# A hybrid decoder layer: the causal mask of the attention scores set by GpSimd's selections in SBUF, in place of identity products in PSUM

## The chip, the cores and the metric

The kernel runs on one core of a Trainium2 chip. Five engines work side by side, each through its own queue in order: TensorE (PE; its weight loads are shown apart, as PEld), VectorE (DVE), ScalarE (ACT), GpSimd (POOL) and SyncE (SP), which here issues the transfers. They wait for each other through semaphores. The metric is the time of the whole kernel on the device in microseconds, the median of several runs.

## The reference

One decoder layer on 512 tokens of 1024 channels: a half-step SwiGLU, a mixer of two halves that read the same normed input (a gated linear recurrence on 512 channels, stick-breaking attention with 8 heads of 64), an output projection, and a second half-step SwiGLU. What the change touches is the attention:

```
z = q @ k.T                                   # one head, one block of 128 queries
causal = k_pos[None, :] < q_pos[:, None]      # a key strictly before the query
log_beta = log_sigmoid(z)
log_1m = where(causal, log_sigmoid(-z), 0.0)
tail = cumsum(log_1m, reverse=True) - log_1m  # what the later keys left of the stick
w = where(causal, exp(log_beta + tail), 0.0)
out = w @ v
```

The weight of a key is thus sigmoid(z) times the product of sigmoid(-z) over the keys between it and the query. A key at or after the query has weight 0 and breaks nothing off: its sigmoid(-z) counts as 1.

## The kernel before

All matrix products are taken in three parts (high by high, high by low, low by high), so that float32 precision is kept; the helper `mm3` issues the three. The layer goes in stages: the first SwiGLU, the projections and the recurrence, the attention together with both halves of the output projection, the second SwiGLU. PE works nearly without a pause through all of them.

The attention (lines 566 to 705) has 24 steps. The heads go in pairs, and a pair goes in three units: query block 3 (512 keys), query block 2 (384 keys), and blocks 1 and 0 together (256 and 128 keys). `weigh` (line 575) computes a unit for both heads: PE forms the scores of each block in a PSUM bank `pz` from three products (line 589; each head has 64 rows of the array, so the two heads' products run beside each other). Then PE adds the mask: an identity in bf16 times the tile `fut_b` adds -1e30 to the last 128 columns of a block where the key is at or after the query (line 598). ScalarE turns the bank into `s` = sigmoid(-z) (line 603; two buffers) and `be` = sigmoid(z) (line 605; five buffers). DVE scans `s` from the last key backwards by multiplication into `rest` (line 608), one scan for each block, and multiplies `be` by it (line 618). With -1e30 in PSUM `s` is 1 and `be` is 0 for the keys that don't count.

`turn_weights` (line 621) transposes a head's weights on PE (line 626) and ScalarE copies them into `wt` (line 636). `attend` (line 639) multiplies them by the values, and `take` (line 651) prepares the result for the output projection (`yal`, line 656, on DVE; the squares, line 160, on ScalarE, summed on POOL, line 161).

The order is written out by hand in part. WEIGH names the steps behind which the next unit's scores are issued; FILL those behind which a block of the recurrent half's output projection fills PE: `project_out` (line 555), whose weights are split by ScalarE (line 121) and DVE (`l_o`, line 123), whose result DVE scales (`yo`, line 563) and POOL adds to x (line 564); REST names the steps that the last such blocks wait for. When the kernel is built, a planner works through all instructions with costs of its own and a priority by the order of the program, and lays down the order of each engine's queue; so each queue's order can change when instructions come or go.

The constants are made at the start (lines 90 to 112): `fut` is a zero tile in which POOL sets -1e30 by one selection (line 106), and DVE casts it and the identity to bf16 (lines 110 and 112).

Of the kernel before, what the change touches and what calls it, by code (L numbers as in the profile page):

```python
# [12 lines left out]
ALU = mybir.AluOpType  # L13
# [14 lines left out]
RG_C = 8.0  # L28
CHUNKS = [8, 7, 7]  # blocks of the hidden width between two partial down projections
WARM = 9  # products that only start the tensor engine's clock  # L30
# Attention goes in 24 steps, each of which turns a block row of one head's weights. The
# steps behind which the next weights are computed, those behind which a block of the
# recurrent half's output projection fills the tensor engine, and those that the
# blocks left over wait for:
WEIGH = (1, 4, 5, 7, 9, 10, 13, 15, 16, 19)
FILL = (4, 8, 12, 16)
REST = (18, 23, 23)

# columns of the packed per-channel vectors
C_G1, C_GM, C_G2 = 0, 8, 16  # L40
# [6 lines left out]
def hybrid_layer_kernel(  # L47
# [25 lines left out]
    def psum(name, **tags):  # L73
        """The eight PSUM banks, cut into the given tags."""
        if banks:
            banks.pop("stack").close()
        banks["stack"] = ExitStack()
        banks["pool"] = banks["stack"].enter_context(
            tc.tile_pool(name=f"ps_{name}", bufs=1, space=PSUM, reuse_waits="tile")
        )  # L80
        banks["tags"] = tags
# [5 lines left out]
    def bank(name, tag="b"):  # L87
        return banks["pool"].tile([P, T], F32, tag=tag, name=name, bufs=banks["tags"][tag])

# [1 line left out]
    mhalf = const.tile([P, 8], F32, tag="mhalf", name="mhalf")  # L91
# [10 lines left out]
    make_identity(nc, ident)  # L102
    # keys at or after the query
    fut = const.tile([P, P], F32, tag="fut", name="fut")
    nc.vector.memset(fut, 0.0)
    nc.gpsimd.affine_select(
        out=fut, in_=fut, pattern=[[-1, P]], compare_op=ALU.is_gt, fill=-1e30, base=0, channel_multiplier=1
    )
    ident_b = const.tile([P, P], BF16, tag="ident_b", name="ident_b")
    nc.vector.tensor_copy(ident_b, ident)  # L110
    fut_b = const.tile([P, P], BF16, tag="fut_b", name="fut_b")
    nc.vector.tensor_copy(fut_b, fut)

    x = [xpool.tile([P, T], F32, tag=f"x{k}", name=f"x{k}") for k in range(KD)]

# [1 line left out]
    def weights(src, name, n=KD * P):  # L117
# [16 lines left out]

# [1 line left out]
    class Normed:  # L136
# [26 lines left out]
        def rsqrt(self, dim):  # L163
            """[tokens, block] 1/sqrt(mean + eps)."""
            n = self.name
            pt = bank(f"pst_{n}", "y")
            for b in range(NB):
                self.summed = nc.tensor.matmul(  # L168
                    pt[:, b : b + 1],
                    self.acc[:, b * P : (b + 1) * P],  # L170
                    ones[:, 0:1],
                    start=True,
                    stop=True,
                )
            m = stat.tile([P, NB], F32, tag="m", name=f"m_{n}")
            nc.vector.tensor_scalar(
                m, pt[:, 0:NB], 1.0 / dim, EPS, op0=ALU.mult, op1=ALU.add
            )
            r = stat.tile([P, NB], F32, tag="r", name=f"r_{n}")
            nc.gpsimd.tensor_tensor(r, m, mhalf[:, 0:NB], op=ALU.pow)  # L180
            self.r = r

        def spread(self):
            """The same along the free axis, on every partition."""
            n, r = self.name, self.r
            pt = bank(f"psr_{n}", "y")
            for b in range(NB):
                self.spreading = nc.tensor.transpose(  # L188
                    pt[:, b * P : (b + 1) * P], r[:, b : b + 1].to_broadcast([P, P]), ident
                )  # L190
            rb = stat.tile([P, T], F32, tag="rb", name=f"rb_{n}", bufs=1)
            nc.scalar.copy(rb, pt)
            self.rb = rb

# [1 line left out]
    def ffn(name, xn, wg, wu, wd, first, done):  # L196
# [59 lines left out]

    # ================= first FFN =================
    psum("ffn_a", b=6, y=2)
    # the tensor engine's clock rises only after some microseconds of work
    pt = bank("warm")  # L260
# [4 lines left out]
    def first_products():  # L265
        """Channels 0..255, in the order in which x and the weights arrive."""
        with tc.tile_pool(name="first", bufs=1, reuse_waits="tile") as fi:
# [52 lines left out]

    # ================= token mixer =================
    mix = ctx.enter_context(ExitStack())
    mp = mix.enter_context(tc.tile_pool(name="mix", bufs=2, reuse_waits="tile"))

    # -4 log_sigmoid(lambda) per channel, with log1p by its series: u = exp(-|lambda|),
    # v = u / (1 + u) = sigmoid(-|lambda|), w = u / (2 + u) = v / (2 - v).
    lam = vec[:, C_LAM : C_LAM + NJ]
# [33 lines left out]

# [1 line left out]
    rnn = ExitStack()  # L363
# [5 lines left out]
    def project(j, between=None):  # L369
        """[128 channels, tokens] of the input projection, before the norm's factor."""  # L370
        pts = []
        for c, n in ((j, "xr"), (NJ + j, "ga")):
            wh, wl = weights_early(w_rg[c], f"{n}{j}")
            pt = bank(f"p{n}{j}")
            for k in range(KD):
                s = slice(k * P, (k + 1) * P)
                mm3(pt, wh[:, s], wl[:, s], nm.h[k], nm.l[k], k == 0, k == KD - 1)
            pts.append(pt)
            if between and n == "xr":
                between()  # L380
        return pts

    def convolve(j, pr, pg):
# [17 lines left out]
        conv.append((xc, xch, xcl))  # L401
        # gelu(g) = g * sigmoid(2 sqrt(2/pi) (g + 0.044715 g^3))
        g2 = rp.tile([P, T], F32, tag="g2", name=f"g2{j}")
# [8 lines left out]
    def gate(j):  # L412
# [5 lines left out]
        mm3(px, bxh[:, s], bxl[:, s], xch, xcl, True, True)  # L418
        # a = exp(-s), tau = tanh(s / 2): sqrt(1 - a^2) = sqrt(tau) (1 + a)
        nc.scalar.activation(dec[:, j, :], pa, AF.Sigmoid, bias=v1(C_BA + j))  # L420
# [11 lines left out]
    def recur():  # L432
        # one change of the activation tables for each function
        with tc.issue_after(box["gate"].ins):
# [26 lines left out]

# [1 line left out]
    qkT = {}  # L463
# [89 lines left out]

# [1 line left out]
    def project_out(k, c, yh, yl, norm, tag, after=None):  # L555
# [9 lines left out]

# [1 line left out]
    # A head's weights are held as [keys, queries], a block of 128 keys every W columns,  # L567
    # from the first query block that sees it on.
    W = 3 * P
    with tc.tile_pool(name="att", bufs=2, reuse_waits="tile") as ap:  # L570
# [4 lines left out]
        def weigh(qbs, pair):  # L575
            """What each key gets: its part of the stick, of what the later keys left."""
            pzs = [bank(f"pz{qbs[0]}_{h}", "z") for h in pair]
            col = 0
            parts = []
            for qb in qbs:  # L580
# [4 lines left out]
                for a, b in (("qh", "kh"), ("qh", "kl"), ("ql", "kh")):  # L585
                    with tc.issue_after(both.ins) if both else nullcontext():
                        for pz, h in zip(pzs, pair):
# [5 lines left out]
                                start=a + b == "qhkh",  # L593
                                stop=False,
                            )
                # from the query on: weight 0, nothing broken off
                for pz in pzs:
                    nc.tensor.matmul(pz[:, col + n - P : col + n], ident_b, fut_b, start=False, stop=True)
                col += n
            for pz, h in zip(pzs, pair):  # L600
# [4 lines left out]
                nc.scalar.activation(be[:, :col], pz[:, :col], AF.Sigmoid)  # L605
                rest = ap.tile([P, T], F32, tag="rest", name=f"rest{u}")
                for c, n in parts:
                    nc.vector.tensor_tensor_scan(
                        rest[:, c : c + n - 1][:, ::-1],
                        s[:, c + 1 : c + n][:, ::-1],  # L610
                        zero.to_broadcast([P, n - 1]),
                        1.0,
                        op0=ALU.mult,
                        op1=ALU.add,
                    )
# [23 lines left out]
        def attend(pair, py, ws):  # L639
            """[channels of the pair, queries]; the heads in different columns of the array"""  # L640
            for b in range(NB):
# [59 lines left out]
        for k in range(KD):  # L701
            # the norm's own small products go ahead of all but the first blocks
            after = None if k < 2 else na.summed if k == 2 else na.spreading
# [3 lines left out]

    # ================= second FFN =================
    psum("ffn_b", b=6, y=2)
# [9 lines left out]
def _layout(x, ffn1_norm, ffn1_w_gate, ffn1_w_up, ffn1_w_down, mix_norm, w_in,  # L719
# [8 lines left out]
    def by_block(w):  # L728
        # [K, N] -> [N/128][p, k, m]: stationary blocks of 128 columns
        k, n = w.shape  # L730
# [59 lines left out]
```

## Time and profile before

| | us |
|---|---|
| median of three runs | 957.67 (957.35 to 958.53) |
| span of the profiled execution, first to last instruction | 953.7 |
| PE busy in the span | 938.0 (98%), 4267 products |
| DVE busy | 524.2 (55%) |
| ACT busy | 331.3 (35%) |
| POOL busy | 124.3 (13%) |

For the profiled execution only its span is known; the median of the timed runs is 4.0 us above it. The profile holds every instruction with its engine, its line, the tiles that it writes and reads, its start and its duration, the idle time of its engine in front of it and what ended that. Busy time of PE counts a product from its start to its modelled end, and products overlap, so a busy PE is not PE at its peak. Durations of POOL are rough. Where several equal instructions follow each other, the timeline puts them in one row with their count, and the duration is that of the whole row.

### The profile page before, as it was taken

How to read it: one execution, taken by the hardware profiler on the slowest of the kernel's cores; microseconds unless marked ns; L12 is line 12 of the kernel's file. 1: busy time of each engine (PE TensorE's matmuls, PEld its weight loads, DVE VectorE, ACT ScalarE, POOL GpSimd, SP SyncE). 2: the span in 40 equal slices, each digit the busy share in tenths (PEclk: the TensorE clock that was granted, in tenths of full speed). 3: DMA queues.
4: the chain of work that ended last, by engine and by line, in shares of the span. 5: the costliest groups of instructions: out<-in, count | busy, mean ns of one | idle time of the engine just before them, and what ended most of it. 6: DMA issues, size and time to landing. Idle time of an engine off the chain costs nothing. (4 is left out here: it accounts for less than half of the span.)

```text
span 953.7 us, 10714 instructions
## 1 busy us (share of the span) xinstructions
PE 938.0 (98%) x4267; PEld 764.9 (80%) x4267; DVE 524.2 (55%) x679; ACT 331.3 (35%) x476; POOL 124.3 (13%) x87
## 2 busy tenths in 40 slices
PE   8999999999999999999899998999999999999998
PEld 6888888888888888888776576888888888888887
DVE  7655334554354556765859949554534545345542
ACT  7232222322222244346456645322212222222220
POOL 4000000000000022552911239100000000000000
PEclk9999999999999999999999999999999999999999
DMA  7222322222322233222110013223232232322331
GB/s 243 92 108 90 109 89 93 106 78 100 111 96 100 78 103 111 96 91 79 67 56 12 24 66 126 96 94 106 71 128 89 91 101 59 131 107 89 95 115 55
DMA packets 29425, 89.32 MB, mean 94 GB/s; under 512 B 3392, under 2 KB 5696, under 8 KB 29376
## 3 DMA queue, kind: packets, MB, share of 16 engines
q1 hardware_dynamic: 29376, 88.65, 27.0%
q8 instruction: 33, 0.54, 0.2%
q14 instruction: 16, 0.13, 0.0%
HBM read 86.54 MB, written 2.10 MB: 93 GB/s over the span
## 5 line engine op out<-in xcount | busy, mean ns | idle before, releaser
L132 PE MATMUL pgb<-xl_b,h_gb 128*128 128x512 f32 x176 | 68.9, 392 | 2.8 <-DVE xl_b L147 2.7
L132 PE MATMUL pdb<-hlb,h_db 128*128 128x512 f32 (+1 forms) x183 | 69.4, 381 | 0.0
L133 PE MATMUL pdb<-hhb,l_db 128*128 128x512 f32 (+1 forms) x183 | 69.1, 381 | 0.0
L132 PE MATMUL pub<-xl_b,h_ub 128*128 128x512 f32 x176 | 69.0, 392 | 0.0
L133 PE MATMUL pub<-xh_b,l_ub 128*128 128x512 f32 x176 | 69.0, 392 | 0.0
L131 PE MATMUL pdb<-hhb,h_db 128*128 128x512 f32 (+1 forms) x183 | 68.9, 381 | 0.0
L131 PE MATMUL pub<-xh_b,h_ub 128*128 128x512 f32 x176 | 68.9, 391 | 0.0
L133 PE MATMUL pgb<-xh_b,l_gb 128*128 128x512 f32 x176 | 68.7, 391 | 0.0
L131 PE MATMUL pgb<-xh_b,h_gb 128*128 128x512 f32 x176 | 68.7, 390 | 0.0
L132 PE MATMUL pda<-hla,h_da 128*128 128x512 f32 x176 | 68.1, 389 | 0.0
L133 PE MATMUL pda<-hha,l_da 128*128 128x512 f32 x176 | 67.8, 389 | 0.0
L131 PE MATMUL pda<-hha,h_da 128*128 128x512 f32 x176 | 67.7, 389 | 0.0
L131 PE MATMUL pga<-xh_a,h_ga 128*128 128x512 f32 x160 | 62.4, 390 | 0.0
L132 PE MATMUL pua<-xl_a,h_ua 128*128 128x512 f32 x160 | 62.3, 390 | 0.0
L133 PE MATMUL pga<-xh_a,l_ga 128*128 128x512 f32 x160 | 62.3, 389 | 0.0
L131 PE MATMUL pua<-xh_a,h_ua 128*128 128x512 f32 x160 | 62.3, 389 | 0.0
L133 PE MATMUL pua<-xh_a,l_ua 128*128 128x512 f32 x160 | 62.2, 389 | 0.0
L132 PE MATMUL pga<-xl_a,h_ga 128*128 128x512 f32 x160 | 62.2, 389 | 0.0
L161 POOL TENSOR_TENSOR sqa_m<-sqa_m,sq_m 128x512 f32<-128x512 f32 x7 | 11.4, 1626 | 330.4 <-issue 312.1
L248 DVE SCALAR_TENSOR_TENSOR x<-pdb,x 128x512 f32<-128x512 f32 (+1 forms) x25 | 16.6, 669 | 68.6 <-PE pdb L133 68.6
L121 ACT CAST h_ga<-r_ga 128x1024 fp32r<-128x1024 f32 x24 | 25.3, 1053 | 79.6 <-issue 34.4
L227 DVE TENSOR_TENSOR uub<-pub,rb_b 128x512 f32<-128x512 f32 x22 | 15.2, 691 | 67.4 <-PE pub L133 67.4
(278 smaller groups left out, 2101.3 us busy)
## 6 DMA issues: line engine op xcount, KB each, us to landing
r_gb<-in_wg SPq DMA_DIRECT2D x22, 512.0 KB, 3.1
r_ub<-in_wu SPq DMA_DIRECT2D x22, 512.0 KB, 3.2
r_ga<-in_wg SPq DMA_DIRECT2D x20, 512.0 KB, 3.2
r_ua<-in_wu SPq DMA_DIRECT2D x20, 512.0 KB, 3.1
r_da<-in_wd SPq DMA_DIRECT2D x16, 448.0 KB, 3.3
r_db<-in_wd SPq DMA_DIRECT2D x16, 448.0 KB, 3.3
r_da<-in_wd SPq DMA_DIRECT2D x8, 512.0 KB, 3.5
r_o<-in_w_out SPq DMA_DIRECT2D x16, 256.0 KB, 2.5
```

Of the source, the lines that this page charges most:

```text
L121: nc.scalar.copy(hi, raw)
L131: nc.tensor.matmul(out_, wh, ah, start=start, stop=False)
L132: nc.tensor.matmul(out_, wh, al, start=False, stop=False)
L133: nc.tensor.matmul(out_, wl, ah, start=False, stop=stop)
L161: nc.gpsimd.tensor_add(self.acc, self.acc, sq)
L227: nc.vector.tensor_mul(u, pu, rb)
L248: nc.vector.scalar_tensor_tensor(x[k][:, t], pt[:, t], 0.5, x[k][:, t], op0=ALU.mult, op1=ALU.add)
```

## The change

The tiles `fut`, `ident_b` and `fut_b` go, and with them a memset, a selection and two casts at the start, and the mask's products in `weigh`; the last of the three score products now closes the bank. When ScalarE has written a head's `s` and `be`, POOL sets the last 128 columns of each block in both tiles by an affine selection in place: where the key is not before the query, `s` becomes 1 and `be` becomes 0. The scans and multiplications then follow as they did. (Comments that the change drops are left out here.)

```diff
-    fut = const.tile([P, P], F32, tag="fut", name="fut")
-    nc.vector.memset(fut, 0.0)
-    nc.gpsimd.affine_select(
-        out=fut, in_=fut, pattern=[[-1, P]], compare_op=ALU.is_gt, fill=-1e30, base=0, channel_multiplier=1
-    )
-    ident_b = const.tile([P, P], BF16, tag="ident_b", name="ident_b")
-    nc.vector.tensor_copy(ident_b, ident)
-    fut_b = const.tile([P, P], BF16, tag="fut_b", name="fut_b")
-    nc.vector.tensor_copy(fut_b, fut)
...
                                 start=a + b == "qhkh",
-                                stop=False,
+                                stop=a + b == "qlkh",
                             )
-                for pz in pzs:
-                    nc.tensor.matmul(pz[:, col + n - P : col + n], ident_b, fut_b, start=False, stop=True)
                 col += n
...
                 rest = ap.tile([P, T], F32, tag="rest", name=f"rest{u}")
+
+                for c, n in parts:
+                    for t, fill in ((s, 1.0), (be, 0.0)):
+                        d = t[:, c + n - P : c + n]
+                        nc.gpsimd.affine_select(
+                            out=d, in_=d, pattern=[[-1, P]], compare_op=ALU.is_gt,
+                            fill=fill, base=0, channel_multiplier=1,
+                        )
                 for c, n in parts:
                     nc.vector.tensor_tensor_scan(
```

## Rows read from the trace of the kernel before

**Rows 1.** The page: its first line, the busy time of each engine with share and count, and the span in 40 equal slices of 23.8 us (each digit the busy share in tenths; PEclk the granted clock).

```profile
span 953.7 us, 10714 instructions
PE 938.0 (98%) x4267; PEld 764.9 (80%) x4267; DVE 524.2 (55%) x679; ACT 331.3 (35%) x476; POOL 124.3 (13%) x87
...
PE   8999999999999999999899998999999999999998
...
DVE  7655334554354556765859949554534545345542
...
POOL 4000000000000022552911239100000000000000
PEclk9999999999999999999999999999999999999999
```

**Rows 2.** A table of the attention by stretch: the stretch and its length, then for PE, PEld, DVE, ACT and POOL in this order the busy us and the instructions in brackets, then the granted clock, the share of the transfer engines and GB/s. The first row is the whole stage.

```profile
497.40:553.50 56.10, 52.60 (x323) 34.77 (x323) 51.33 (x79) 39.07 (x91) 10.75 (x8) 1.00 0.07 24
497.40:507.00 9.60, 7.70 (x54) 4.70 (x54) 8.33 (x10) 6.66 (x15) 1.70 (x2) 1.00 0.08 27
507.00:524.00 17.00, 16.86 (x101) 11.38 (x101) 16.55 (x30) 11.88 (x29) 2.28 (x2) 1.00 0.05 16
524.00:538.00 14.00, 12.57 (x82) 7.92 (x81) 12.02 (x16) 10.11 (x24) 3.93 (x3) 1.00 0.11 39
538.00:549.00 11.00, 10.97 (x64) 6.88 (x63) 10.25 (x15) 6.28 (x16) 1.64 (x1) 1.00 0.05 19
```

**Rows 3.** The same table over the stage, for the scans of line 608 alone and for the multiplications of line 618 alone (DVE).

```profile
497.40:553.50 56.10, 27.33 (x32) 1.00 0.07 24
...
497.40:553.50 56.10, 17.87 (x32) 1.00 0.07 24
```

**Rows 4.** Who waited for whom in the stage: the waiting engine, tile and line, whom it waited for, the us in total, the number of waits and the longest.

```profile
ACT s L603 <- DVE rest L608: 6.8, 8, 1.8
...
PE pw L626 <- DVE be L618: 3.2, 3, 1.5
...
DVE rest L608 <- ACT s L603: 2.6, 4, 1.0
```

**Rows 5.** The timeline of the first microseconds: the first and the last of DVE's steps for the mask's constants, and ScalarE's first work on an input.

```profile
1.01 0.17 DVE L105 MEMSET fut<- 128x128 f32 x1
...
1.57 0.23 DVE L112 CAST fut_b<-fut 128x128 bf16<-128x128 f32 x1
...
4.29 0.72 ACT L145 ACTIVATE xh_a<-x,vec 128x512 fp32r<-128x512 f32 x1 [2.07 <-DMA x<-in_xT]
```

**Rows 6.** The mask's products: all of them (shortest, median and longest in ns, first and last start), their busy time in the stage on PE and PEld, and PE's timeline around the first pair of them.

```profile
L598 PE MATMUL pz<-fut_b,ident_b x32: 219/224/230, 498.4 to 549.1; 128*128 128x128 bf16 x32
...
497.40:553.50 56.10, 4.56 (x32) 1.82 (x32) 1.00 0.07 24
...
497.80 0.40 PE L589 MATMUL pz<-kTl,qTh 64*128 64x512 f32 x2
498.03 0.40 PE L589 MATMUL pz<-kTh,qTl 64*128 64x512 f32 x2
498.36 0.29 PE L598 MATMUL pz<-fut_b,ident_b 128*128 128x128 bf16 x2
498.58 0.44 PE L589 MATMUL pz<-kTh,qTh 64*128 64x384 f32 x1
```

**Rows 7.** Groups of POOL's instructions by line and form: busy us, mean ns of one, idle time before them. First the two selections of the whole kernel, then the additions to x in the stage.

```profile
masks.py:199 POOL TENSOR_SCALAR_AFFINE_SELECT ident<-ident 128x128 f32<-128x128 f32 x1 | 0.3, 293 | 0.1
L106 POOL TENSOR_SCALAR_AFFINE_SELECT fut<-fut 128x128 f32<-128x128 f32 x1 | 0.3, 292 | 0.0
...
L564 POOL TENSOR_TENSOR x<-x,yo 128x512 f32<-128x512 f32 x5 | 8.2, 1648 | 39.7 <-DVE yo L563 39.7
```

**Rows 8.** The timeline of POOL and of DVE around 514 us: a POOL instruction with two inputs beside DVE instructions with two inputs in SBUF. The multiplication of the same form at 500.59 stands last, for comparison; POOL was idle then.

```profile
513.71 1.64 POOL L564 TENSOR_TENSOR x<-x,yo 128x512 f32<-128x512 f32 x1 [8.98 <-DVE yo L563]
...
513.55 0.68 DVE L123 TENSOR_TENSOR l_o<-r_o,h_o 128x512 fp32r<-128x512 f32 x1
514.14 1.76 DVE L618 TENSOR_TENSOR be<-be,rest 128x511 f32<-128x511 f32 x1
...
500.59 0.69 DVE L618 TENSOR_TENSOR be<-be,rest 128x511 f32<-128x511 f32 x1
```

**Rows 9.** The same around 391 us, where POOL's instruction has one input tensor (line 406), and all instructions of line 406 (shortest, median and longest in ns).

```profile
389.61 0.77 POOL L390 TENSOR_SCALAR xc<-xr,vec 128x512 f32<-128x512 f32 x1 [6.21 <-DVE xr L386]
390.85 0.80 POOL L406 TENSOR_SCALAR g<-g 128x512 f32<-128x512 f32 x1 [0.47 <-ACT g L404]
...
390.41 0.75 DVE L394 SCALAR_TENSOR_TENSOR xc<-xr,vec,xc 128x512 f32<-128x512 f32 x1 [0.32 <-POOL xc L390]
...
391.20 0.98 DVE L394 SCALAR_TENSOR_TENSOR xc<-xr,vec,xc 128x512 f32<-128x512 f32 x1
...
L406 POOL TENSOR_SCALAR g<-g x4: 619/800/1182, 390.8 to 417.9; 128x512 f32<-128x512 f32 x4
```

**Rows 10.** The timeline of the stage, rows of ACT, DVE and POOL that show how one waits for the other: the first unit, a sum of squares, and the last double unit.

```profile
498.63 0.60 ACT L603 ACTIVATE s<-pz 128x512 f32<-128x512 f32 x1 [0.67 <-PE pz L598]
...
499.26 1.22 DVE L608 TENSOR_TENSOR_SCAN rest<-s,zero 128x511 f32<-128x511 f32 x1 [0.57 <-ACT s L603]
...
499.60 0.61 ACT L603 ACTIVATE s<-pz 128x512 f32<-128x512 f32 x1
...
501.19 1.22 DVE L608 TENSOR_TENSOR_SCAN rest<-s,zero 128x511 f32<-128x511 f32 x1
...
534.67 0.60 ACT L160 ACTIVATE sq_t<-py 128x512 f32<-128x512 f32 x1 [1.39 <-DVE yal L656]
...
535.34 1.27 POOL L161 TENSOR_TENSOR sqa_t<-sqa_t,sq_t 128x512 f32<-128x512 f32 x1 [1.79 <-ACT sq_t L160]
...
549.26 0.49 ACT L603 ACTIVATE s<-pz 128x384 f32<-128x384 f32 x1
549.65 0.49 ACT L605 ACTIVATE be<-pz 128x384 f32<-128x384 f32 x1
...
549.79 1.00 DVE L608 TENSOR_TENSOR_SCAN rest<-s,zero 128x255 f32<-128x255 f32 x2 [0.23 <-ACT s L603]
```

## The prediction

> **What bounds the kernel now.** I read the page first: its busy shares and its strip of 40 slices [rows 1]. TensorE (PE) is busy for 98% of the span, at a granted clock of nine tenths or more in every slice, that is at 2.4 GHz. It is the only engine near its limit over the whole kernel. But the share is a mean. VectorE (DVE) is at 55% overall but at nine tenths in the two slices (501 to 548 us) that hold most of the attention, where GpSimd (POOL) is at one and two tenths. So I read the attention alone, as a table by stretch [rows 2]. In its 56.10 us PE is busy for 52.60 and DVE for 51.33, and PE's clock stands at 1.00. The idle time of PE lies in two stretches (1.90 us in the first, 1.43 in the third), that of DVE is 4.77 in all. The two engines are within 1.3 us of each other, so this stage has no spare engine but ACT (39.07) and POOL (10.75). What DVE does there is almost all scans (27.33 us) and the multiplications behind them (17.87) [rows 3], exactly the work that the change touches.
>
> Then the waits of the stage [rows 4]. ScalarE waits 6.8 us for a scan to give back one of the two `s` buffers, PE waits 3.2 us for `be` from a multiplication, and DVE waits 2.6 us (4 times) for `s`. DVE is waited for more than it waits. The path goes to and fro: DVE paces from 497 to 507 and from 524 to 538, where PE stands idle, PE in the stretches between, where it doesn't [rows 2], and at the end the last scans and turns pace again. Whatever is added to DVE in this stage shows within about a microsecond; what is taken from PE shows only as far as DVE has idle time to give back.
>
> **The change part by part.** *The constants.* `fut`, `ident_b`, `fut_b` go: one memset, one selection and two casts between 1.0 and 1.8 us. The first input is not there before 4.29 us (ScalarE's first scaled copy starts there, after a wait for its load), so this is worth nothing [rows 5].
>
> *The identity products.* 32 products go (8 heads times 4 query blocks), each with its weight load. They have 4.56 us of busy time, at 0.22 us each, and overlap. In time on PE a pair of heads costs 0.22 us: the pair starts at 498.36 and the next product at 498.58 [rows 6]. The load of the identity also sits idle until the 64-row products before it are through: the last of these start at 498.03, and such products follow each other at 0.23 us (497.80, 498.03; all in [rows 6]), so without the pair the next could start at 498.26 in place of 498.58, 0.32 us sooner. 16 pairs times 0.22 to 0.32 are 3.5 to 5.1 us of PE. ScalarE's `s` can start sooner by the same amount.
>
> *The selections.* In their place come 64 (8 heads, 4 blocks, `s` and `be`), each 128 by 128 f32 in place on POOL. The trace has this very instruction twice, at 0.29 us [rows 7]. 64 times 0.29 are 18.7 us; POOL goes from 10.75 to about 29.4 of 56.1 us, far from a bound. The price is what they do to DVE. Where POOL runs beside a DVE instruction with two SBUF inputs, the trace shows turns, not sharing [rows 8]: POOL adds to x from 513.71 to 515.35; the subtraction that DVE had begun keeps its 0.68 us, the multiplication that starts at 514.14 takes 1.76 in place of 0.69, 1.07 more, for an overlap of 1.21. So DVE loses the overlap less 0.14, and for a whole selection at most 0.29 less 0.14, 0.15 us. Nearer to a selection are POOL's instructions with one input [rows 9]. The one at 390.85 ends at 391.65; DVE's at 391.20 takes 0.98 in place of 0.75, so it loses 0.23 of an overlap of 0.45. Its base is 0.62 (its shortest), and it ended 0.49 behind the DVE instruction that it had waited for, so 0.13 of it passes in the wait. By these a waiting selection ends 0.29 - 0.13 = 0.16 us after DVE's instruction, and the next of DVE would lose 0.16 less 0.22, nothing. The bounds are thus 0 and 0.15 us for each; the far end is its whole 0.29. I take 0.06, nearer to the row with one input: 64 times 0.06 = 3.8 us, bounds 0 and 9.6.
>
> The Trainium skill (SBUF — State Buffer, section Who interferes with whom) states that a DVE instruction with two SBUF inputs and a GpSimd instruction that reads SBUF exclude each other, and that whichever issues second blocks fully until the first is done. The turns in [rows 8] agree, with 1.07 us lost of 1.21. By that rule without any overlap the 64 selections would cost 18.7 us in place of 3.8, an estimate of 976 us for the kernel.
>
> *The new wait.* The scan no longer waits for ScalarE alone but for POOL behind it. Behind a waiting scan stand, in DVE's order, its multiplication, the next head's scan, and the `l_o` and `yo` steps of the output projection that fills PE; PE's turns wait for them. Most of this is hidden: `s` is usually there 1 to 2 us before its scan (done at 500.21 for the scan at 501.19) [rows 10]. Where DVE already waits for `s`, the selection adds POOL's start 0.07 us after ScalarE's end (535.27, 535.34), 0.29 for itself and DVE's start 0.03 later (390.38, 390.41 in [rows 9]), some 0.39 us in place of 0.03 (499.23, 499.26), and the removed products give 0.22 to 0.32 back: up to 0.14 for each of 4 waits, 0.5 us. In the double unit (blocks 1 and 0) POOL's order is `s`, `be`, `s`, `be`: the second scan waits for the third selection, which stands behind a `be` that ScalarE delivers 0.39 us after `s` (549.26, 549.65), while DVE scanned both blocks in 1.00 us without a pause. For 8 heads: 0 if ScalarE is ahead, three selections at 0.16 plus 0.10 = 0.58 if not; I take 0.2, 1.6 us (bounds 0 and 4.6). Selections also queue behind the five additions to x, 1.65 us each, that POOL runs in the stage [rows 7]; DVE loses most of those already today, so only the selection itself comes on top: 0 to 5 times 0.29, I take 0.5 us.
>
> *What is given back.* DVE has 4.77 us of idle time. Of this the waits for `s` shrink when DVE comes later or PE sooner. In the stretches that PE paces, DVE's idle time is 0.45 and 0.75 us [rows 2], so at most 1.2 of PE's gain passes on; in 524 to 538 it is 1.98, which added work partly fills. I take 2.8 back of 4.77; the start of the stage (0.57) and the short gaps of 0.1 us between a scan and its own multiplication remain.
>
> *Sum.* 3.8 + 0.5 + 1.6 + 0.5 - 2.8 = +3.6 us, with bounds of about -3 (no loss to the turns, no exposed wait, 3 us given back) and +15. The profiled execution has a span of 953.7 us, the median of the three runs is 957.67, 4.0 us more that lie around the span and don't change. 957.7 + 3.6 = 961.3 us.
>
> **The rivals.** *PE's gain wins (faster).* If a selection fits into the gap of 0.1 us that DVE leaves between a scan and its multiplication (500.48 in [rows 10], 500.59 in [rows 8]), and into DVE's instructions that read PSUM, DVE loses nothing, and the earlier `s` takes away most of DVE's waits. DVE's 51.33 us plus some 1.8 of unavoidable gaps are then the floor, 53.1 in place of 56.1: -3 us, 954.7. For it speaks the one-input row; against it that DVE's gaps are few and that PE's own wait is only 3.5 us. It decides when a selection costs DVE under about 0.02 us and no scan waits. *A draw.* The added DVE time of 3 to 4 us is met by idle time and by the shorter PE queue; 957.7, within 1.9. *DVE is shut out for longer.* If each selection costs 0.15, as the two-input rows would have it, 5.8 us more than in my sum: 967.1; up to 976 at the whole 0.29. For it speaks that most DVE work in the stage has two SBUF inputs, the scan among them; against it the smaller loss beside one-input instructions. The skill's rule, named above, is this rival without the overlap. *It does not shorten PE.* If the change from 64-row to 128-row weights costs the same behind the scores anyway, PE gains 0.22 and not 0.32 for a pair; as DVE paces, that moves the sum by under 1 us and stays in the forecast. The order of all queues is laid out again by the planner when the kernel is built; a different place for a block of output projection could move any of these by 1 to 2 us, and the range holds that.
>
> **How the numbers follow.** Forecast, DVE paces and loses some: 0.45, at 961.3. Shut out for longer: 0.13, at 967. Draw: 0.22. PE's gain wins: 0.20, at 954.7. A measurement of this kernel can tell about 0.2% (1.9 us) from no change. So slower has 0.58, same 0.22, faster 0.20. The range goes from 955.0 to 968.0: it leaves out the lower half of the fast case (0.1) and the upper half of the shut-out case with a rest of the forecast (0.1). Within the forecast alone it would be 959.6 to 965.
>
> **What would show it.** In the changed profile: 64 selections on POOL near 0.29 us when alone and up to over 1 us where they wait behind a scan; scans and multiplications that are longer than their shortest by 0.05 to 0.15 in the mean (now 27.33 and 17.87 us in sum); DVE's waits named after POOL's selections in place of ScalarE; PE's wait for `be` above 3.2 us; the stage longer than 56.1 by 3 to 4 us, and nothing outside it changed. The forecast is wrong if DVE's sum in the stage stays below 53, if PE's idle time in it falls, or if the loss comes from POOL's queue (scans waiting behind additions to x) and not from turns with DVE.

## The result, and the profile after

The changed kernel takes 959.21 us (median of 20 runs, 958.44 to 961.44), the kernel before 957.66 in the same comparison (20 runs, 955.52 to 959.24). The ratio is 1.0018, with a 95% interval of 1.0012 to 1.0025: about 1.7 us slower (1.1 to 2.4 by the interval). The forecast was 3.6 us slower.

The two profiled spans differ by more, 957.0 against 953.7. The later runs list span and time of each execution side by side, and they differ by 1.7 to 1.9 us in every one (957.0 and 958.70 for the profiled execution of the changed kernel). By that the profiled execution of the kernel before took about 955.5 us, 2.2 below its median, and the 4.0 us that the prediction put around the span were 1.8 and an execution that was quicker than most. So the size of the loss is read from the ratio, and the profiles show where it lies.

The page of the changed kernel, its first lines and two rows of the strip of 40 slices:

```profile
span 957.0 us, 10763 instructions
...
PE 939.4 (98%) x4235; PEld 766.2 (80%) x4235; DVE 526.6 (55%) x676; ACT 331.4 (35%) x476; POOL 159.3 (17%) x150
...
DVE  7655434544345556756859859554534545445542
...
POOL 4000000000000022542918759200000000000000
```

POOL has 35 us more, 34 of them in the attention. The attention by stretch, columns as in [rows 2]:

```profile
497.10:555.40 58.30, 52.34 (x290) 34.55 (x290) 52.37 (x77) 37.78 (x87) 45.06 (x71) 0.97 0.07 23
497.10:507.00 9.90, 7.60 (x46) 5.17 (x46) 8.40 (x10) 6.58 (x15) 7.71 (x11) 0.90 0.07 26
507.00:524.00 17.00, 16.74 (x92) 11.21 (x90) 16.69 (x29) 11.52 (x28) 13.97 (x25) 0.96 0.05 16
524.00:538.00 14.00, 12.19 (x68) 7.66 (x68) 11.04 (x14) 8.64 (x20) 8.61 (x11) 1.00 0.11 39
538.00:549.00 11.00, 9.66 (x53) 6.34 (x51) 9.84 (x16) 8.26 (x21) 9.70 (x18) 1.00 0.01 1
```

The stage is 58.30 us long in place of 56.10. PE has 33 products fewer in it (the 32 of the mask, and one of the output projection that falls behind the stage's end) and is idle for 5.96 us in place of 3.50: part of what it saved it waits. DVE works for 52.37 us in place of 51.33 and is idle for 5.93 in place of 4.77. Its added work is larger than that difference, since the stage now holds five of the output projection's scalings (`yo`) in place of six, some 0.7 us. Behind the stage 401.6 us follow in place of 400.2 in the two profiled executions; what makes up these 1.4 us isn't shown. The scans alone and the multiplications alone, to be read against [rows 3]:

```profile
497.10:555.40 58.30, 30.25 (x32) 0.97 0.07 23
...
497.10:555.40 58.30, 16.05 (x32) 0.97 0.07 23
```

The scans are busy for 2.9 us more and the multiplications for 1.8 us less. In part that is because POOL's additions to x, which lengthen the DVE instruction that they fall on by about 1 us [rows 8], now fall on scans and no longer on multiplications. POOL is marked busy for 45.06 us, far above the 10.75 before plus 64 times 0.29; its groups say why (line 598 is the new selection; busy us, mean ns of one, idle time before):

```profile
L598 POOL TENSOR_SCALAR_AFFINE_SELECT be<-be 128x128 f32<-128x128 f32 x32 | 19.0, 606 | 0.4 <-ACT be L592 0.4
L598 POOL TENSOR_SCALAR_AFFINE_SELECT s<-s 128x128 f32<-128x128 f32 x32 | 17.6, 560 | 4.5 <-ACT s L590 4.5
```

A selection takes 0.56 to 0.61 us in the mean and 0.29 when alone [rows 7]: I read the other half as waiting for its turn beside DVE. The waits of the stage, to be read against [rows 4] (603 is the scan, 613 the multiplication, 590 and 592 ScalarE's `s` and `be`):

```profile
ACT s L590 <- DVE rest L603: 11.8, 14, 1.5
DVE rest L603 <- POOL s L598: 4.7, 4, 2.3
...
PE po L121 <- ACT be L592: 2.3, 3, 1.6
PE pz L579 <- ACT be L592: 2.0, 3, 1.1
...
PE pw L621 <- DVE be L613: 1.0, 2, 0.8
```

DVE now waits for POOL and not for ScalarE, 4.7 us in place of 2.6. ScalarE waits longer for a scan to give back an `s` buffer (11.8 in place of 6.8), and through it PE waits for a free score bank (2.3 and 2.0 us), and hardly for `be` any more (1.0 in place of 3.2).

The longest of DVE's waits, 2.27 us, in the timeline of ACT, POOL and DVE:

```profile
536.82 0.60 ACT L150 ACTIVATE sq_t<-py 128x512 f32<-128x512 f32 x1 [1.00 <-DVE yal L651]
537.31 0.49 ACT L590 ACTIVATE s<-pz 128x384 f32<-128x384 f32 x1
...
537.49 1.28 POOL L151 TENSOR_TENSOR sqa_t<-sqa_t,sq_t 128x512 f32<-128x512 f32 x1 [3.23 <-ACT sq_t L150]
538.73 0.54 POOL L598 TENSOR_SCALAR_AFFINE_SELECT s<-s 128x128 f32<-128x128 f32 x2
...
539.05 1.11 DVE L603 TENSOR_TENSOR_SCAN rest<-s,zero 128x255 f32<-128x255 f32 x2 [2.27 <-POOL s L598]
539.22 1.03 POOL L598 TENSOR_SCALAR_AFFINE_SELECT be<-be 128x128 f32<-128x128 f32 x2
540.09 0.73 DVE L613 TENSOR_TENSOR be<-be,rest 128x255 f32<-128x255 f32 x2
```

`s` is done at 537.80, but its selection stands behind the sum of squares on POOL until 538.73. The same place cost 1.04 us before, by another road (the scan waited for an `s` that ScalarE had queued behind those squares). POOL's order in this double unit is both selections on `s`, then both on `be`; the same order stands in all eight. And the last scan row shows the price of the turns: the pair of scans takes 1.11 us where it took 1.00 [rows 10], about 0.05 more for each instruction.

### The profile page after: what moved, and what is told of

It is laid out like the page before. It is cut to its first block, busy times and chain, and to the rows that moved or that the text cites. A ratio compares the mean times of both kernels' runs of the same rounds, so it can differ in the third digit from the quotient of the medians.

```text
span 957.0 us, 10763 instructions
## 1 busy us (share of the span) xinstructions
PE 939.4 (98%) x4235; PEld 766.2 (80%) x4235; DVE 526.6 (55%) x676; ACT 331.4 (35%) x476; POOL 159.3 (17%) x150
```

## The experiments

Theory A: DVE paces the stage; a selection costs it a turn at the shared SBUF read, and what PE saves passes on only in part. Rival B: PE paces, and the loss is the scan's wait for POOL, not what a turn takes from DVE's own instructions. Rival C: the planner's new order of the queues. All ratios are to the kernel before on the same chip; 0.001 is 0.96 us.

**The removal alone.** Edit of the changed kernel:

```diff
-                for c, n in parts:
-                    for t, fill in ((s, 1.0), (be, 0.0)):
...
-                        nc.gpsimd.affine_select(
```

> The changed kernel without its 64 selections: no mask at all is applied, neither in PSUM nor in SBUF (the weights of later keys are left in), so this times the removal of the identity products alone. Theory A (DVE paces the stage; a selection costs it a turn at the shared SBUF read, and PE's gain passes on only as far as DVE has idle time): 955 to 957 us, a gain of 1 to 3 on the kernel before, well under the 3.5 to 5.1 us that PE saves. Rival B (PE paces; the selections' wait is the whole loss): 952.5 to 954. Rival C (the planner's new order of the queues is the loss): 957.5 to 960, no gain, since the order changes here too.

Measured: 0.9979 (0.9968 to 0.9991), 954.64 us. The removal gains 2.0 us, as A has it, and rival B's figure of 3.5 or more is outside. C expected no gain, which is outside too.

**The selections alone.** The same lines added to the kernel before.

> The kernel before with the 64 selections added on top of the identity products (the mask is set twice): times the selections alone. Theory A: DVE paces, so giving PE its products back costs little: 959 to 961 us, 0 to 1.5 above the changed kernel. Rival B (PE paces): the 3.5 to 5.1 us of products come on top, 962.5 to 964. Rival C (order): between 957 and 962 without a pattern.

Measured: 1.0030 (1.0019 to 1.0040), 959.52 us: 2.9 us for the selections on top of the products, only 1.2 above the changed kernel, and the two intervals overlap. B's 3.5 us or more above the changed kernel are outside. The products are cheap where DVE paces.

**The same waits without reading.**

```diff
-                        d = t[:, c + n - P : c + n]
-                        nc.gpsimd.affine_select(
...
+                        nc.gpsimd.memset(t[:, c + n - P : c + n], fill)
```

> The changed kernel with a memset in the place of each selection, on the same columns and in the same chain of waits: POOL writes without reading SBUF. The whole last block of 128 keys is masked, not only its upper triangle. Theory A (turns at the shared read): the turns go, scans and multiplications keep their shortest durations beside POOL's memsets, and the time falls to 956 to 957.8 us. Rival B (the wait for POOL's queue, not the turns): the waits stay, and the time stays at 958.7 to 959.5. Rival C: anything in 957 to 960, with the scans' durations still lengthened.

Measured: 0.9987 (0.9978 to 0.9997), 955.57 us. With the same order of waits, but a POOL instruction that doesn't read, 3.0 of the 3.7 us between the kernel with no mask and the changed one are gone: POOL's reading of SBUF is the main cause. B as it was stated expected no gain and is wrong. But the links of the chain are shorter too: a memset takes 0.20 us on POOL, a selection beside DVE 0.56 to 0.61, and DVE waits for POOL for 0.7 us (`s`) and 1.2 (`be`) here, 4.7 (`s`) in the changed kernel. So this run alone doesn't divide the 3.0 us between longer DVE instructions and longer waits for POOL. The rest, 0.8 us between this kernel and the one with no mask, is what the shorter waits leave, and the intervals overlap. DVE's groups in the stage of this kernel (busy us, mean ns of one, idle before):

```profile
L599 DVE TENSOR_TENSOR_SCAN rest<-s,zero 128x511 f32<-128x511 f32 x8 | 9.7, 1213 | 0.7 <-POOL s L597 0.7
...
L609 DVE TENSOR_TENSOR be<-be,rest 128x511 f32<-128x511 f32 x8 | 5.5, 683 | 0.6 <-DVE be L609 0.3
L599 DVE TENSOR_TENSOR_SCAN rest<-s,zero 128x255 f32<-128x255 f32 x8 | 5.4, 674 | 0.0
...
L609 DVE TENSOR_TENSOR be<-be,rest 128x255 f32<-128x255 f32 x8 | 3.2, 405 | 1.2 <-POOL be L597 1.2
L599 DVE TENSOR_TENSOR_SCAN rest<-s,zero 128x127 f32<-128x127 f32 x8 | 3.2, 396 | 0.0
...
L609 DVE TENSOR_TENSOR be<-be,rest 128x127 f32<-128x127 f32 x8 | 2.2, 277 | 0.0
```

and the same groups of the changed kernel:

```profile
L603 DVE TENSOR_TENSOR_SCAN rest<-s,zero 128x511 f32<-128x511 f32 x8 | 10.2, 1270 | 2.3 <-POOL s L598 2.3
L603 DVE TENSOR_TENSOR_SCAN rest<-s,zero 128x255 f32<-128x255 f32 x8 | 6.1, 765 | 2.5 <-POOL s L598 2.5
L613 DVE TENSOR_TENSOR be<-be,rest 128x511 f32<-128x511 f32 x8 | 6.0, 746 | 0.5
...
L603 DVE TENSOR_TENSOR_SCAN rest<-s,zero 128x127 f32<-128x127 f32 x8 | 3.6, 446 | 0.0
L613 DVE TENSOR_TENSOR be<-be,rest 128x255 f32<-128x255 f32 x8 | 3.4, 428 | 0.0
...
L613 DVE TENSOR_TENSOR be<-be,rest 128x127 f32<-128x127 f32 x8 | 2.7, 332 | 0.0
```

Form by form (scans over 511, 255 and 127 columns, then multiplications over the same) the reading selections add 57, 91, 50, 63, 23 and 55 ns to one instruction: 56 ns in the mean, 2.7 us over these 48 instructions. The forms over 383 columns are left out because additions to x fall on them, and on different ones in the two kernels.

**A second selection for each.**

```diff
-                        nc.gpsimd.affine_select(
+                        for _ in range(2):
+                            nc.gpsimd.affine_select(
```

> The changed kernel with every selection issued twice, 128 in all. Theory A: each further selection costs DVE another turn of 0.06 to 0.08 us and the chain another 0.29 us where DVE waits: 64 times 0.07 = 4.5, so 962 to 965 us. Rival B (only the exposed waits count, some 4 to 8 of them at 0.29): 960 to 962. Rival C: no pattern, 958 to 961.

Measured: 1.0168 (1.0151 to 1.0184), 972.31 us. A's upper end was 965, B's 962: no theory had this. The first 64 cost 3.7 us, the next 64 cost 14.4, 0.22 each. The stage (all engines as in [rows 2]), PE's and DVE's waits, and four rows of POOL's and DVE's timelines:

```profile
497.10:570.10 73.00, 57.95 (x293) 37.38 (x293) 57.27 (x79) 39.87 (x92) 66.89 (x136) 0.91 0.06 19
```

```profile
PE pw L622 <- DVE be L614: 13.8, 9, 3.8
DVE rest L604 <- POOL s L599: 12.5, 19, 4.2
```

```profile
507.36 1.43 POOL L599 TENSOR_SCALAR_AFFINE_SELECT s<-s 128x128 f32<-128x128 f32 x3
508.74 1.09 POOL L599 TENSOR_SCALAR_AFFINE_SELECT be<-be 128x128 f32<-128x128 f32 x3
...
507.68 1.02 DVE L604 TENSOR_TENSOR_SCAN rest<-s,zero 128x383 f32<-128x383 f32 x1 [0.43 <-POOL s L599]
509.06 0.62 DVE L614 TENSOR_TENSOR be<-be,rest 128x383 f32<-128x383 f32 x1 [0.36 <-POOL be L599]
```

The stage is 14.7 us longer than the changed kernel's. DVE works for 4.9 us more in it (with one split and one scaling more of the output projection) and is idle for 15.73 us in place of 5.93: two thirds of the further loss is waiting, and only a third is longer work. For POOL's `s` alone the scans wait 12.5 us in place of 4.7. POOL is marked busy for 66.89 of 73.00 us and paces. The stage has 64 scans and multiplications; my reading is that 64 selections find a turn beside them, while with 128 DVE runs out of released work, as in the 0.36 and 0.43 us above. It was not separated further; PE's granted clock is lower in this stage too (0.91, 0.97 in the changed kernel's), which may be a part.

**Half of them, and shorter ones.** Only the selections on `s`; then 64 selections over 16 columns.

```diff
-                    for t, fill in ((s, 1.0), (be, 0.0)):
+                    for t, fill in ((s, 1.0),):
```

> The changed kernel with the 32 selections on s alone; those on be are left out (the weights of keys at or after the query are not set to zero). Theory A, turns: the 64 selections together cost 3.7 us (the changed kernel against the one with no mask), so half of them cost about half: a ratio to the kernel before of 0.999 to 1.000, 956 to 957.7 us. Rival B, the wait: DVE waits for the selections of s alone, so all of the loss stays, ratio 1.0015 to 1.002. Rival C, order: no pattern.

```diff
-                        d = t[:, c + n - P : c + n]
+                        d = t[:, c + n - 16 : c + n]
...
-                            out=d, in_=d, pattern=[[-1, P]], compare_op=ALU.is_gt,
-                            fill=fill, base=0, channel_multiplier=1,
+                            out=d, in_=d, pattern=[[-1, 16]], compare_op=ALU.is_gt,
+                            fill=fill, base=16 - P, channel_multiplier=1,
```

> The changed kernel with 64 selections over the last 16 columns of each block in place of 128 (the rest of the mask is left out). Theory A by columns (a turn holds DVE as long as POOL reads): the cost falls to nearly that of the memsets, ratio 0.998 to 0.9995. Theory A by count (each turn has a fixed price): 1.001 to 1.002. Rival B: the waits stay, 1.000 to 1.001.

Measured: 0.9992 (0.9982 to 1.0002), 956.27 us, for the half, a third of the cost for half the selections (a half lies within the interval too); 0.9995 (0.9983 to 1.0008), 956.24 us, for the short ones, 1.5 of 3.7 us. The half fits A, and B's 1.0015 or more is outside. For the short ones "by count alone" (1.001 to 1.002) is outside; "by columns alone" ended at 0.9995, and B's 1.000 to 1.001 overlaps with the interval, so neither is excluded. A short selection takes 0.19 us at its shortest, but in the mean those on `s` are marked busy for 0.55 us, as long as before, and those on `be` for 0.43 in place of 0.61. DVE is not lengthened by them: scans over 255 columns take 675 ns and multiplications over 127 columns 274, as beside the memsets. Their rows on POOL:

```profile
L598 POOL TENSOR_SCALAR_AFFINE_SELECT s<-s 128x16 f32<-128x16 f32 x32 | 17.3, 552 | 6.3 <-ACT s L590 5.9 <-PE pw L621 0.4
L598 POOL TENSOR_SCALAR_AFFINE_SELECT be<-be 128x16 f32<-128x16 f32 x32 | 13.4, 432 | 0.6 <-ACT be L592 0.5
```

**One selection for the double unit.** Its two masked blocks adjoin, so one selection can cover both: 48 in all, over the same columns.

```diff
+                c0, n0 = parts[0]
+                    d = t[:, c0 + n0 - P : col].rearrange("p (b k) -> p b k", k=P)
...
+                        out=d, in_=d, pattern=[[0, len(parts)], [-1, P]], compare_op=ALU.is_gt,
```

> The changed kernel, complete, with one selection over both adjoining blocks of the double unit in place of two: 48 selections over the same columns. Theory A by the count of turns: three quarters of 3.7 us, ratio 1.0005 to 1.001; by the columns that a turn holds: nearly as the changed kernel, 1.0013 to 1.002. Rival B: the second scan of the double unit no longer waits behind the selection of be, which would give back most of the 0.8 us of waits: 1.0005 to 1.001 with the scans' durations unchanged.

Measured: 1.0016 (1.0006 to 1.0025), 958.64 us, no different from the changed kernel. A by columns held (1.0013 to 1.002); by count and B (both 1.0005 to 1.001) reach into the interval only at its lower end. There was little to gain for B: in the changed kernel POOL's queue already had both selections on `s` ahead of those on `be` (538.73 and 539.22 above), so the second scan didn't stand behind a `be`.

**The turns without the wait.** In the kernel before, 64 selections that read `s` and `be` and write to tiles that nobody reads.

```diff
+                        scr = ap.tile([P, P], F32, tag=f"scr{m}", name=f"scr{m}{u}_{i}")
+                        nc.gpsimd.affine_select(
+                            out=scr, in_=t[:, c + n - P : c + n], pattern=[[-1, P]], compare_op=ALU.is_gt,
```

> The kernel before, with its identity products, plus 64 selections that read the same 128 columns of s and be and write to tiles that nobody reads: the turns at DVE's second read without any wait of a scan for POOL. Theory A (turns): most of the loss of the selections is there: ratio to the kernel before 1.002 to 1.003, near the kernel that sets the mask twice (1.0030). Rival B (the scan's wait for POOL): no loss, 0.9995 to 1.0005.

Measured: 1.0057 (1.0041 to 1.0072), 962.49 us, above what A expected and far above B. No scan waits for POOL here, but the edit brings other waits for it: ScalarE can't reuse an `s` buffer before POOL has read it,

```profile
ACT s L603 <- POOL scrs L610: 7.1, 7, 1.8
```

and the multiplications wait 1.5 us until POOL has read `be`. So this kernel takes away one wait for POOL and adds two; it decides nothing between A and B.

**A version with fewer turns.** The mask of `be` set on the turned weights instead, one selection for each head over its four diagonal blocks, and 24 selections on `s`.

```diff
+            for w in ws:
+                d = w.rearrange("p (b c) -> p b c", b=NB)[:, :, :P]
+                nc.gpsimd.affine_select(
+                    out=d, in_=d, pattern=[[0, NB], [1, P]], compare_op=ALU.is_gt,
+                    fill=0.0, base=0, channel_multiplier=-1,
+                )
             py = bank(f"py{j}", "y")
             attend(pair, py, ws)
```

> A version that computes the whole layer with fewer selections: 24 on s (one for each unit of a head) ahead of the scans, and in place of those on be 8 on the turned weights, one for each head over its four diagonal blocks of 128, behind ScalarE's copy and ahead of the products with the values. Theory A: 32 turns and none of them between a scan and its multiplication by need: ratio 0.998 to 1.000, it may beat both kernels. Against it: the products with the values now wait for POOL, 0.6 us for each head, and an addition to x in front of it adds up to 1.6: 1.001 to 1.003 if PE has nothing to do meanwhile.

Measured: 1.0019 (1.0009 to 1.0028), 959.02 us. It saves nothing on the changed kernel, and A's 0.998 to 1.000 is missed. The loss has another face here. The multiplications are as short as beside memsets (402 ns over 255 columns, 276 over 127), but DVE waits for the selections on `s` nearly as long as in the changed kernel, with 32 selections in place of 64:

```profile
DVE rest L602 <- POOL s L597: 4.4, 5, 1.7
```

So waits for POOL can cost as much as longer DVE instructions do, and the count of turns alone doesn't tell the time. How much of this loss is that wait wasn't separated.

**POOL's additions moved to DVE.** If turns are the price, POOL's two-input additions to x are dear: 1.07 us of DVE for the one in [rows 8], against 0.68 us that one takes on DVE in the stage of the first run below.

```diff
-        nc.gpsimd.tensor_add(x[k], x[k], tmp)
+        (nc.vector if c == 0 else nc.gpsimd).tensor_add(x[k], x[k], tmp)
```

In the kernel before:

> The kernel before, complete, with the additions to x of the recurrent half's output projection (8, most of them in the attention) on DVE in place of POOL. Theory A: one such addition takes 1.65 us on POOL and shuts DVE out for 1.08 us, while DVE's own two-input instruction of that size takes 0.60 more: 6 in the stage save 2.9 us of DVE, ratio 0.997 to 0.999. Rival: DVE's time is not what ends the stage, then 1.000 to 1.001.

In the changed kernel:

> The changed kernel with the same additions on DVE, so that POOL has the selections and the squares alone and no selection stands behind an addition. Theory A: as there, and the selections' queue is shorter: 1.5 to 3 us less than the changed kernel, ratio 0.9985 to 1.0005 to the kernel before. Rival: 1.0015 to 1.0025, as the changed kernel.

And all 16 of them, in the kernel before:

> The kernel before, complete, with all 16 additions to x of the output projection on DVE, those of the attention half too (they lie from 572 to 597 us, where POOL's additions stretch the splits of line 147 from 0.74 to 1.78 us). Theory A: the further 8 save DVE 0.4 us each there, but PE is fed by others in that stretch: ratio 0.996 to 0.9975, equal to or a little under the kernel with 8 moved. Rival: DVE becomes the bound of that stretch, 0.998 to 1.000.

Measured: 0.9974 (0.9963 to 0.9984), 955.24 us; 1.0010 (1.0000 to 1.0019), 958.16 us; 0.9971 (0.9961 to 0.9980), 955.24 us. The kernel before gains 2.5 us with 8 additions on DVE, as A has it, and no more with all 16. The changed one gains less, 0.8 us against its own 1.0018 where A had 1.5 to 3, and the two intervals overlap, so that run decides nothing. The stage of the kernel before with 8 moved: all engines as in [rows 2], then DVE's multiplications alone, then its scans alone:

```profile
497.30:552.10 54.80, 52.36 (x323) 34.77 (x323) 49.64 (x84) 39.07 (x91) 2.47 (x3) 1.00 0.07 25
...
497.30:552.10 54.80, 14.40 (x32) 1.00 0.07 25
...
497.30:552.10 54.80, 25.68 (x32) 1.00 0.07 25
```

The same 32 scans and 32 multiplications take 40.1 us in place of 45.2 [rows 3], and DVE, which now does the additions as well, is busy for 1.7 us less. This version and the one with all 16 moved are the quickest of the whole layer found.

## Why the prediction was right, and where its sizes were off

*What bounds the stage.* Right. DVE paces: PE lost the mask's 32 products and waits 2.5 us more; the kernel with both masks costs only 1.2 us over the changed one, though PE has all its products back; and work taken from DVE (the additions) shortens the kernel by 2.5 us.

*The turns.* 64 times 0.06 = 3.8 us was forecast. The six forms differ by 0.02 to 0.09 us with and without reading, 0.056 in the mean, and in time reading costs 3.0 us (changed kernel against memsets). The size is right, in part by luck: the one-input row gave nothing, the two-input rows 0.15, and 0.06 was a choice between them. That POOL's reading costs this is shown. How the 3.0 us divide is not: the six forms are 2.7 us longer in sum, and the waits for POOL are longer as well, since a selection that waits for its turn comes later. The rival of a longer shut-out (0.15 each) is wrong for the first 64. It doesn't come back with the second 64 either: they cost 0.22 each in time, but DVE's work grows by at most 0.08 each, and the rest is idle time of DVE. The Trainium skill (SBUF — State Buffer, section Who interferes with whom) says that the second to issue blocks fully and that a POOL instruction which only writes doesn't contend with a two-input one. The memsets agree with the latter. The former fits the long addition, with 1.07 us lost of an overlap of 1.21, better than the selections: beside one DVE lost 0.06 us of 0.29, and beside a short one, of 0.19 us, nothing. Why a short turn costs so little isn't shown.

*The new waits.* This is the step that was mis-sized. The prediction had 0.5 + 1.6 + 0.5 = 2.6 us; measured are 0.8 (memsets against no mask), not clear of zero, with links that are shorter than a selection's. The largest part, 1.6 us for the second scan of the double unit, is the error. It rested on POOL's order `s`, `be`, `s`, `be`, the order of the program; the planner laid out `s`, `s`, `be`, `be` in all eight double units (538.73, 539.22), so that wait couldn't arise. The part for selections queued on POOL exists, and its longest wait stands behind a sum of squares (the scan at 539.05), not behind an addition to x.

*What is given back.* 2.8 us taken. The removal alone gave 2.0 (0.9 to 3.1); with the selections there, taking away the products gave 1.2 (changed kernel against both masks). With the terms -2.0 + 0.8 + 3.0 the sum is +1.8, and the result +1.7, but that is no test of them: each is the difference between two kernels of a chain that ends at the changed one.

*The signs that it named.* Selections between 0.29 and over 1 us, longer scans, DVE's waits named after POOL: seen. PE's wait for `be` above 3.2 us: wrong, it fell to 1.0, since PE waits earlier, for a score bank. The stage longer by 3 to 4 us and nothing outside it changed: 2.2, and 1.4 more behind it. DVE's sum above 53: not reached, 52.37. One `yo` of 0.7 us moved out of the stage (with it the sum would be 53.1), and the multiplications fell from 17.87 to 16.05, where additions to x had fallen on them before; about half of the stage's added length shows as idle time of DVE (1.16 of 2.2 us). By its own words this sign spoke against the forecast; the memsets speak for the reading as the cause, and leave room for the waits.

*Order of the queues (rival C).* Every kernel here has an order of its own, so C can't be excluded as a part of any one difference. As the cause it would give no pattern, and the costs rise with what POOL reads: nothing (0.9979, memsets 0.9987), 64 selections over 16 columns or 32 over 128 (0.9995 and 0.9992, the same within their intervals), 64 over 128 (1.0018), 128 of them (1.0168). The version with fewer turns (1.0019) stands outside that pattern. What one order is worth against another was not tried.

## What to carry to other kernels

Where DVE is nearly full, ask of every POOL instruction beside it whether it reads SBUF, and price it by the turns that DVE loses and by the waits behind it, not by its own duration: the short ones here cost DVE 0.06 us each at one to each DVE instruction, while a 512-column addition with two inputs cost it more than doing it itself. Where a planner lays out the queues, read the order of a queue from the trace before pricing a wait by the order of the program. Work that is taken from PE is worth only what the engine that paces the stage can give back. And compare spans only with the spread of the runs beside them: here one profiled execution lay 2.2 us below its median, more than the effect.

## What the runs showed of the hardware

The changed kernel's profile has a stretch at the lower clock inside the attention; the granted clock is the third figure from the right (stretch, PE, PEld, DVE, ACT, POOL, clock, share of the transfer engines, GB/s):

```profile
502.00:503.00 1.00, 0.41 (x1) 0.10 (x1) 1.00 (x2) 0.41 (x2) 0.83 (x2) 1.00 0.00 0
503.00:504.00 1.00, 0.48 (x4) 0.45 (x5) 1.00 (x3) 0.94 (x3) 0.85 (x2) 1.00 0.00 0
504.00:505.00 1.00, 1.00 (x9) 0.45 (x5) 1.00 (x2) 0.33 (x1) 1.00 (x1) 1.00 0.00 0
505.00:506.00 1.00, 0.46 (x2) 0.41 (x2) 1.00 (x1) 0.54 (x2) 1.00 (x2) 0.54 0.00 0
506.00:507.00 1.00, 1.00 (x3) 0.75 (x3) 1.00 (x3) 0.46 (x2) 1.00 (x2) 0.50 0.00 0
507.00:508.00 1.00, 1.00 (x4) 0.66 (x3) 1.00 (x3) 0.90 (x3) 1.00 (x3) 0.50 0.00 0
508.00:509.00 1.00, 1.00 (x7) 0.91 (x6) 0.99 (x3) 0.28 (x1) 1.00 (x3) 0.76 0.00 0
```

PE was busy for 0.41 and 0.48 us of the microseconds from 502 and from 503, waiting for ScalarE to free a score bank, and its clock was at 1.2 GHz in place of 2.4 from about 505 to 508.5. The profile of before has no such stretch in the attention, though PE is idle for 1.90 us at the same place; what made the clock fall here isn't shown. It is not what the change costs: seven runs of the changed kernel with a mean clock of 0.996 took 958.51 to 959.72 us, 959.3 in the mean, and 66 runs of the kernel before at that same clock, in the later comparisons, 956.7. The stage with memsets had a lower clock (0.94) than the changed kernel's (0.97), and that kernel is quicker. But the clock goes with the scatter: 14 runs of the kernel before at 0.993 took 958.7 in the mean.
